# Linear attention: the newest gates' cumulative sum, moved behind the slot's outputs and queued behind the two parts of the decayed state

## The chip, the cores and the metric

The kernel runs on one core of a Trainium2 chip. A core has a matrix engine (PE in the profile; PEld is its weight load), a vector engine (DVE), a scalar engine (ACT), GpSimd (POOL, hardly used here) and SyncE (SP), which issues the DMAs. Each engine runs its own list of instructions, and semaphores order them against each other. The metric is the device time of one execution in microseconds (us).

## What is computed

One layer of an encoder block on a sequence of 1024 tokens, width 1024: a projection, a gated linear attention in both directions (GLA), a windowed attention (SWA), their output projections and a feed-forward block. The change lies in the GLA. Cut to it, the reference reads:

```python
def _gla_direction(q, k, v, log_g, include_diag):
    ...
    b = jnp.cumsum(log_g, axis=3)
    b_last = b[:, :, :, -1:, :]
    q_dec = q * jnp.exp(b)
    k_inv = k * jnp.exp(-b)
    k_tail = k * jnp.exp(b_last - b)
    scores = jnp.where(mask, jnp.einsum("bhncd,bhnmd->bhncm", q_dec, k_inv), 0.0)
    o_intra = jnp.einsum("bhncm,bhnme->bhnce", scores, v)
    chunk_kv = jnp.einsum("bhnmd,bhnme->nbhde", k_tail, v)
    def step(state, inp):
        kv_n, dec_n = inp
        return dec_n[..., None] * state + kv_n, state
    _, states = lax.scan(step, ...)
    o_inter = jnp.einsum("bhncd,nbhde->bhnce", q_dec, states)
    return (o_intra + o_inter).reshape(bsz, s, dv)
```

The gates are `log_g = max(log_sigmoid(z) / 16, -0.5)`. There are four heads, with 128 key and 256 value channels.

## The kernel before

**Number format.** Matrix products of full precision are made of three fp32r products: each operand is split into a high part (ACT copies it to fp32r) and a low part (DVE subtracts the high part), and `mm3` (L75) multiplies high by high, high by low and low by high. So nearly every operand costs one ACT and one DVE instruction before PE can use it.

**Slots.** The GLA runs as a software pipeline of slots t (loop at L627). Chunks of 128 tokens are numbered n = 8*head + c over the four heads, and go in pairs (even c and the next). What is done for chunk n stands in these slots:

- slot n, even n: `g_gates` (L399) for the pair. PE multiplies the gates' codes to `z`; ACT takes an exponential (L419), DVE clips it (L420), ACT takes the logarithm (L421), and DVE forms the cumulative sum along the tokens (L422, a scan of 128x512) and the three small rows `sm` from it (L425, L426) that give the chunks' decays.
- same slot, recorded last: `g_decays` (L430). DVE subtracts the reference points (L437, L438), ACT takes two exponentials in place (L440, L441), DVE multiplies them with k and q (`en` L443, and `G` L444). `G` has one buffer.
- slot n+1, recorded last: `g_parts` (L446): the high and low parts `kh`, `kl`, `q2f`, `q2b`.
- slot n+3: `g_scores` (L458): transposes of `en`, parts `kth` and `ktl` of them (L475, L476), the scores, ACT's copy `sp` of them (L483), the masked copy (L484), and the parts `sh` and `sl` (L487, L488).
- slot n+4: `g_out` (L493) for each chunk, in four steps: six matmuls to `kv` (128x256 each); DVE's new state `pf` (L502, or L506 at a head's first chunk), ACT's copy `kb` of the other direction (L504); the **decayed state's two parts**, `th` on ACT (L514) and `tl` on DVE (L515); and the output `o`, made of `sh`, `sl` and, from the second chunk on, the previous chunk's `th` and `tl`, which ACT copies to `ob` (L522).
- later slots: `g_back_out` (L539) and `g_back` (L524) run the other direction backwards (`thb` L533, `tlb` L534, `kb` L536, `ob` L544), and `g_turn` (L559) transposes the outputs (`ot`, L565).

Between these stages `fill` (L258) puts matmuls of the other projections: 34 in a slot up to t = 7, 21 up to t = 23, 18 up to t = 35, then 11 (`GF`, L24). Their weights need `wh` (ACT, L67) and `wl` (DVE, L69). DVE also has `x_sums` (L576, L581), side work for a later stage.

**What sets the order.** PE's order is the order in which the code is written (`manual_schedule`, L625). The order on ACT, DVE and SP is decided at build time by a scheduler that starts from the recorded order; at run time each of these engines takes its instructions in that fixed order. PSUM tiles of the GLA come from a ring of four buffers (`chtile`, L49): a new one can be written when the one four before it has been read.

Of the kernel before, what the change touches and what calls it, by code (L numbers as in the profile page):

```python
# [8 lines left out]
F32 = mybir.dt.float32  # L9
FR = mybir.dt.float32r  # L10
U32 = mybir.dt.uint32
AF = mybir.ActivationFunctionType
ALU = mybir.AluOpType
# [6 lines left out]
NC = 8  # L20
# [10 lines left out]
def body(tc, i, out):  # L31
    nc = tc.nc
    with ExitStack() as root:
# [15 lines left out]
        def chtile(shape, dt=F32):  # L49
            return psc.tile(list(shape), dt, tag="ch", name=nm("ch"))  # L50
# [21 lines left out]
        def mm(o, a, b, start, stop):  # L72
            nc.tensor.matmul(o, a, b, start=start, stop=stop)  # L73

        def mm3(o, ah, al, bh, bl, start, stop):  # L75
            mm(o, ah, bh, start, False)
            mm(o, ah, bl, False, False)
            mm(o, al, bh, False, stop)
# [191 lines left out]
        def need(key):  # L270
            while key not in scr:
                fill(12)
# [118 lines left out]
        def gtile(tag, shape=(P, 256), dt=F32, bufs=2):  # L391
            return gt.tile(list(shape), dt, tag=tag, name=nm(tag), bufs=bufs)
# [2 lines left out]
            pass  # L395

        gla = {}

        def g_gates(hd, c):  # L399


            pr = Chunk()
            for j in range(2):
                a = gla[hd, c + j] = Chunk()
                a.pr, a.j, a.t = pr, j, slice(j * P, (j + 1) * P)
            s, co = c // 4, (c % 4) * P
            for nme in ("q", "k"):
                need((f"{nme}{hd}", s))
            qk = gtile("qk", (P, 2, 256))
            nc.sync.dma_start(out=qk[:, 0], in_=scr[f"q{hd}", s][:, co:co + 256])  # L410
            nc.sync.dma_start(out=qk[:, 1], in_=scr[f"k{hd}", s][:, co:co + 256])
            z = chtile((P, 2, 256))
            for d in range(2):
                mm(z[:, d], upS[:, d, hd * P:(hd + 1) * P], lrS[:, c * P:(c + 2) * P], True, True)
            G = gtile("G", (P, 4, 2, P), bufs=1)
            Gt = G.rearrange("p a j t -> p a (j t)")
            Gf = G.rearrange("p a j t -> p (a j t)")
            cs, e, csf, ef = G[:, 0:2], G[:, 2:4], Gf[:, 0:512], Gf[:, 512:1024]
            nc.scalar.activation(ef, z.rearrange("p d t -> p (d t)"), AF.Exp, scale=-1.0)  # L419
            nc.vector.tensor_scalar(ef, ef, float(np.expm1(8.0)), None, op0=ALU.min)  # L420
            nc.scalar.activation(ef, ef, AF.Ln, bias=ones[:, 0:1])  # L421
            nc.vector.tensor_tensor_scan(csf, mask.rearrange("p c t -> p (c t)"), ef, 0.0, op0=ALU.mult, op1=ALU.add)  # L422

            pr.sm = gtile("sm", (P, 2, 2, 2), bufs=16)
            nc.vector.tensor_scalar(pr.sm, cs[:, :, :, 63:128:64], -1.0 / 16, None, op0=ALU.mult)  # L425
            nc.vector.tensor_tensor(pr.sm[:, :, :, 1], pr.sm[:, :, :, 1], pr.sm[:, :, :, 0], op=ALU.subtract)  # L426

            pr.qk, pr.G = qk, G

        def g_decays(hd, c):  # L430
            pr = gla[hd, c].pr
            qk, G = pr.qk, pr.G
            Gt = G.rearrange("p a j t -> p a (j t)")
            Gf = G.rearrange("p a j t -> p (a j t)")
            cs, e, csf, ef = G[:, 0:2], G[:, 2:4], Gf[:, 0:512], Gf[:, 512:1024]
            late = bass.AP(Gf.tensor, Gf.offset, [list(Gf.ap[0]), [255, 2], [P, 2], [1, P]])
            nc.vector.tensor_tensor(e, late, cs[:, :, :, 63:64].to_broadcast([P, 2, 2, P]), op=ALU.subtract)  # L437
            nc.vector.tensor_scalar(e[:, 1, :, 0:1], cs[:, 1, :, 63:64], -1.0, None, op0=ALU.mult)  # L438

            nc.scalar.activation(csf, ef, AF.Exp, scale=-1.0 / 16)  # L440
            nc.scalar.activation(ef, ef, AF.Exp, scale=1.0 / 16)  # L441
            pr.en = gtile("en", (P, 2, 256))
            nc.vector.tensor_tensor(pr.en, Gt[:, 1:3], qk[:, 1:2].to_broadcast([P, 2, 256]), op=ALU.mult)  # L443
            nc.vector.tensor_tensor(Gt[:, 0:4:3], Gt[:, 0:4:3], qk[:, 0:1].to_broadcast([P, 2, 256]), op=ALU.mult)  # L444
# [48 lines left out]
        def g_out(hd, c):  # L493

            a = gla[hd, c]
            kv = chtile((P, 2, 256))
            for d in range(2):
                mm3(kv[:, d], a.kth[:, d], a.ktl[:, d], a.vh, a.vl, True, True)
            a.pf = gtile("pf")
            if c:  # L500
                pf, dec, th, tl = a.before
                nc.vector.scalar_tensor_tensor(a.pf, pf, dec[:, 0:1], kv[:, 0], op0=ALU.mult, op1=ALU.add)  # L502
                a.kb = gtile(f"kb{c}", bufs=2 if c < 5 else 1)
                nc.scalar.copy(a.kb, kv[:, 1])  # L504
            else:
                nc.vector.tensor_copy(a.pf, kv[:, 0])  # L506
                a.kb = None
            if c < NC - 1:
                n = gla[hd, c + 1]
                dec2 = gtile("dec", (P, 1))  # L510
                nc.scalar.activation(dec2, n.pr.sm[:, 0, n.j, 0:1], AF.Exp, bias=a.pr.sm[:, 0, a.j, 1:2])
                th2 = gtile("th", dt=FR)
                tl2 = gtile("tl", dt=FR)
                nc.scalar.activation(th2, a.pf, AF.Copy, scale=dec2[:, 0:1])  # L514
                nc.vector.scalar_tensor_tensor(tl2, a.pf, dec2[:, 0:1], th2.bitcast(F32), op0=ALU.mult, op1=ALU.subtract)  # L515
                n.before = a.pf, dec2, th2, tl2
            o = chtile((P, 256))
            mm3(o, a.sh, a.sl, a.vh, a.vl, True, c == 0)
            if c:
                mm3(o, a.pr.q2[0][:, 0, a.t], a.pr.q2[0][:, 1, a.t], th, tl, False, True)  # L520
            a.ob = gtile(f"ob{c}", bufs=2 if c < 5 else 1)
            nc.scalar.copy(a.ob, o)  # L522

        def g_back(hd, c):  # L524

            a = gla[hd, c]
            if c < NC - 1:
                n = gla[hd, c + 1]
                dec = gtile("decb", (P, 1))
                nc.scalar.activation(dec, a.pr.sm[:, 1, a.j, 1:2], AF.Exp, bias=n.pr.sm[:, 1, n.j, 0:1])  # L530
                th = gtile("thb", dt=FR)
                tl = gtile("tlb", dt=FR)
                nc.scalar.activation(th, n.kb, AF.Copy, scale=dec[:, 0:1])  # L533
                nc.vector.scalar_tensor_tensor(tl, n.kb, dec[:, 0:1], th.bitcast(F32), op0=ALU.mult, op1=ALU.subtract)  # L534
                if c:
                    nc.vector.scalar_tensor_tensor(a.kb, n.kb, dec[:, 0:1], a.kb, op0=ALU.mult, op1=ALU.add)  # L536
                a.thb, a.tlb = th, tl
# [74 lines left out]
        for n in range(NH * NC):  # L612
            hd, c = divmod(n, NC)
            cb = hd * NC + NC + 4 + (NC - 1 - c)
            tt = cb + c % 2 + 2
            for j, (t, f) in enumerate(((n, g_gates), (n + 3, g_scores), (n + 4, g_out),
                                        (cb, g_back_out), (tt, g_turn))):
                if j > 1 or c % 2 == 0:
                    at[t, j + (j == 4 and c % 2)] = (f, hd, c)
                last = max(last, t)  # L620
            if c % 2 == 0:
                behind[n] = (g_decays, hd, c)
                behind[n + 1] = (g_parts, hd, c)
# [198 lines left out]
        for n in range(2 * KT):  # L822
            t, g = divmod(n, 2)
# [9 lines left out]
        order = (prep, a_rope, a_scores, a_turn, k_turn, a_out, a_probs)  # L833
# [91 lines left out]
        def pair_T3(f):  # L925
            nme, m, a, b = PAIRS[f]
            g = pend[f]
            product(g.X, wsplit(g.s3, 512), XT["T3"], 4, False, True)
            return result((f"{nme}{m + 4}", 1), g.X, g.p5)
# [69 lines left out]
        with tc.manual_schedule(engines={mybir.EngineType.PE}):  # L999
# [15 lines left out]
            for j in range(0, len(PAIRS), 2):  # L1015
# [4 lines left out]
                v = [pair_T3(f) for f in two]  # L1020
# [561 lines left out]
```

## Time and profile before

| | us |
|---|---|
| time, median of 3 runs (1623.01 to 1624.67) | 1623.91 |
| the profiled execution's own time | 1624.31 |
| its span in the profile | 1622.5 |
| the GLA's slots in it, about | 48 to 338 |
| DVE busy over the span | 1223.9 |
| ACT busy over the span | 915.0 |

The span is 1.8 us shorter than the profiled execution's own time, and that time is 0.4 us above the median. A group of the profile gives source line, engine, operation, output and inputs, shapes, count, busy time and the mean of one instruction in ns, and behind the bar the time for which the engine stood idle just before them and what ended it. A row of the timeline gives the start, the duration and the instruction; brackets give the idle time before it and who ended it. Matmuls are pipelined: one shown with 0.28 us lets the next start after 0.12 us, so waits of PE are read from the distance of the starts.

### The profile page before, as it was taken

To read this page: it belongs to the slowest core of one execution; us is meant where nothing else is said; L and a number is where in the kernel's file an instruction comes from. 1 tells how busy PE (TensorE), PEld (TensorE's weight loads), DVE (VectorE), ACT (ScalarE), POOL (GpSimd) and SP (SyncE) were. 2 spreads that over 40 slices of the span, in tenths; PEclk is the share of its full clock that TensorE was granted. 3 is DMA by queue.
4 is the path that set the end of the run, shared out by engine and by line. 5 is a ranking of instruction groups with operands and counts; after the bars stand their busy time and mean duration, and the time that the engine had idled before them with its cause. 6 is when DMAs were issued, how large, how long until landed. Compare 5 with 4: busy or idle time off the path is not lost.

```text
span 1622.5 us, 23392 instructions
## 1 busy us (share of the span) xinstructions
PE 1611.6 (99%) x7644; PEld 1341.5 (83%) x7644; DVE 1223.9 (75%) x2315; ACT 915.0 (56%) x1883; POOL 0.2 (0%) x4
## 2 busy tenths in 40 slices
PE   9999999999999999999999999999999999999999
PEld 7888888888888888888888888888888888888887
DVE  8568888845999777876855878677777888789655
ACT  7456777873999745445732547754444444354442
POOL 0000000000000000000000000000000000000000
PEclk9999999999999999999999999999999999999999
DMA  8855757878554487878842656643435564695433
GB/s 279 295 180 194 252 172 256 274 264 284 176 162 143 129 268 253 270 242 263 282 126 89 192 192 214 196 141 124 136 121 177 170 219 146 207 328 189 149 98 117
DMA packets 196362, 323.25 MB, mean 199 GB/s; under 512 B 22318, under 2 KB 47790, under 8 KB 196240
## 3 DMA queue, kind: packets, MB, share of 16 engines
q1 hardware_dynamic: 196240, 321.76, 60.8%
q8 instruction: 60, 0.98, 0.2%
q14 instruction: 62, 0.51, 0.1%
HBM read 216.29 MB, written 105.38 MB: 198 GB/s over the span
## 4 chain that ended last, share of the span: by engine, by line
PE 89%; DVE 4%; ACT 3%; DMA 2%; issue 1%; SPq 0%; DVEq 0%; ACTq 0%
PE mm L73 20%; PE mm L877 10%; PE mm L879 10%; PE mm L878 10%; PE mm L1421 7%; PE ch L73 7%; PE ch L1421 6%; PE ch L878 5%; PE ch L879 5%; PE ch L877 5%; PE mm L246 3%; PE ch L783 1%; DMA kvr<-skv 1%; DMA st<-in_xT_dram 1%; DVE wl L69 0%
## 5 line engine op out<-in xcount | busy, mean ns | idle before, releaser
L856 ACT ACTIVATE wh<-ws 128x512 fp32r<-128x512 f32 x164 | 102.9, 629 | 152.5 <-PE mm L878 81.0
L73 PE MATMUL mm<-wh,xh 128*128 128x512 f32 x320 | 127.1, 397 | 0.0
L73 PE MATMUL mm<-wh,xl 128*128 128x512 f32 x320 | 127.1, 397 | 0.0
L73 PE MATMUL mm<-wl,xh 128*128 128x512 f32 x320 | 126.6, 395 | 0.0
L857 DVE TENSOR_TENSOR wl<-ws,wh 128x512 fp32r<-128x512 f32 x164 | 112.2, 686 | 14.0 <-ACT wh L856 13.5
L67 ACT ACTIVATE wh<-wr 128x512 fp32r<-128x512 f32 x118 | 73.5, 627 | 53.0 <-PE mm L73 21.3
L69 DVE TENSOR_TENSOR wl<-wr,wh 128x512 fp32r<-128x512 f32 x118 | 80.8, 686 | 25.2 <-ACT wh L67 22.8
L856 ACT ACTIVATE wh<-a 128x512 fp32r<-128x512 f32 x66 | 41.6, 632 | 89.1 <-PE ch L1421 42.3
L856 ACT ACTIVATE wh<-wr 128x512 fp32r<-128x512 f32 x76 | 47.8, 631 | 58.1 <-PE mm L878 17.6
L857 DVE TENSOR_TENSOR wl<-a,wh 128x512 fp32r<-128x512 f32 x66 | 45.5, 690 | 39.7 <-ACT wh L856 39.3
L1421 PE MATMUL mm<-hh,wl 128*128 128x512 f32 x176 | 68.6, 390 | 0.0
L1421 PE MATMUL mm<-hl,wh 128*128 128x512 f32 x176 | 68.5, 389 | 0.0
L1421 PE MATMUL mm<-hh,wh 128*128 128x512 f32 x176 | 68.5, 389 | 0.0
L73 PEld LDWEIGHTS mm<-wl,xh 128*128 128x128 f32 x320 | 60.2, 188 | 9.8
L73 PEld LDWEIGHTS mm<-wh,xl 128*128 128x128 f32 x320 | 60.2, 188 | 9.6
L73 PEld LDWEIGHTS mm<-wh,xh 128*128 128x128 f32 x320 | 60.3, 188 | 9.1 <-DVE st L141 0.2
L857 DVE TENSOR_TENSOR wl<-wr,wh 128x512 fp32r<-128x512 f32 x76 | 52.0, 685 | 7.8 <-ACT wh L856 7.1
L870 DVE TENSOR_TENSOR ws<-wr,wr 128x512 f32<-128x512 f32 x80 | 54.5, 687 | 4.3 <-DMA wr<-in_w_f_dram 1.7
L1388 DVE TENSOR_TENSOR hl<-hr,hh 128x512 fp32r<-128x512 f32 x77 | 52.8, 686 | 5.7 <-ACT hh L1387 5.4
L1387 ACT ACTIVATE hh<-hr 128x512 fp32r<-128x512 f32 x77 | 47.7, 619 | 9.0 <-DMA hr<-B 5.1
L1421 PE MATMUL ch<-hh,wh 128*128 128x512 f32 x132 | 51.3, 389 | 0.0
L1421 PE MATMUL ch<-hl,wh 128*128 128x512 f32 x132 | 51.3, 389 | 0.0
(454 smaller groups left out, 4984.5 us busy)
## 6 DMA issues: line engine op xcount, KB each, us to landing
wr<-in_w_fi_dram SPq DMA_DIRECT2D x110, 256.0 KB, 3.9
wr<-in_w_f_dram SPq DMA_DIRECT2D x100, 256.0 KB, 3.7
wh<-wh SPq DMA_DIRECT2D x80, 256.0 KB, 3.1
wl<-wl SPq DMA_DIRECT2D x80, 256.0 KB, 3.1
B<-c SPq DMA_DIRECT2D x44, 256.0 KB, 2.1
T<-st SPq DMA_DIRECT2D x44, 256.0 KB, 2.9
a<-in_w_fo_dram SPq DMA_DIRECT2D x44, 256.0 KB, 5.3
hr<-T SPq DMA_DIRECT2D x44, 256.0 KB, 2.7
```

The costliest lines, as they stand in the source:

```text
L67: nc.scalar.activation(h, raw, AF.Copy)
L69: nc.vector.tensor_tensor(l, raw, h.bitcast(F32), op=ALU.subtract)
L73: nc.tensor.matmul(o, a, b, start=start, stop=stop)
L246: nc.tensor.matmul(Y[q], w[:, c], x, start=f0, stop=f1, skip_group_check=True)
L856: nc.scalar.activation(h, src, AF.Copy)
L857: nc.vector.tensor_tensor(l, src, h.bitcast(F32), op=ALU.subtract)
L870: nc.vector.tensor_tensor(t, x, y, op=op)
L877: nc.tensor.matmul(o, h[:, c], x[kk][0], start=start and kk == 0, stop=False, skip_group_check=True)
L878: nc.tensor.matmul(o, h[:, c], x[kk][1], start=False, stop=False, skip_group_check=True)
L879: nc.tensor.matmul(o, l[:, c], x[kk][0], start=False, stop=kk == nk - 1, skip_group_check=True)
L1388: nc.vector.tensor_tensor(l, r, h.bitcast(F32), op=ALU.subtract)
L1421: nc.tensor.matmul(ys[m], a[:, c], b, start=f0, stop=f1, skip_group_check=True)
```

## The change

The scan and the two `sm` instructions leave `g_gates` and open the new `g_sums`, which holds the body of `g_decays`. `g_decays` is recorded where it was, last in the even slot, behind `g_out` of that slot; so the scan is now recorded behind `g_out` too. While `g_sums` is recorded, `issue_after` makes each of its instructions on ACT follow the newest `th` on ACT's queue, and each on DVE follow the newest `tl` on DVE's queue (`state` holds the two; it is empty until the first `g_out`, so the first two pairs have no such edge). No instruction is added or left out.

```diff
         gla = {}
+        state = []
 ...
             nc.scalar.activation(ef, ef, AF.Ln, bias=ones[:, 0:1])
-            nc.vector.tensor_tensor_scan(csf, mask.rearrange("p c t -> p (c t)"), ef, 0.0, op0=ALU.mult, op1=ALU.add)
-
-            pr.sm = gtile("sm", (P, 2, 2, 2), bufs=16)
-            nc.vector.tensor_scalar(pr.sm, cs[:, :, :, 63:128:64], -1.0 / 16, None, op0=ALU.mult)
-            nc.vector.tensor_tensor(pr.sm[:, :, :, 1], pr.sm[:, :, :, 1], pr.sm[:, :, :, 0], op=ALU.subtract)
-
             pr.qk, pr.G = qk, G

         def g_decays(hd, c):
-            pr = gla[hd, c].pr
+            with ExitStack() as order:
+                for v in state:
+                    order.enter_context(tc.issue_after(v.ins))
+                g_sums(gla[hd, c].pr)
+
+        def g_sums(pr):
             qk, G = pr.qk, pr.G
 ...
+            nc.vector.tensor_tensor_scan(csf, mask.rearrange("p c t -> p (c t)"), ef, 0.0, op0=ALU.mult, op1=ALU.add)
+
+            pr.sm = gtile("sm", (P, 2, 2, 2), bufs=16)
+            nc.vector.tensor_scalar(pr.sm, cs[:, :, :, 63:128:64], -1.0 / 16, None, op0=ALU.mult)
+            nc.vector.tensor_tensor(pr.sm[:, :, :, 1], pr.sm[:, :, :, 1], pr.sm[:, :, :, 0], op=ALU.subtract)
+
             late = bass.AP(Gf.tensor, Gf.offset, [list(Gf.ap[0]), [255, 2], [P, 2], [1, P]])
 ...
-                nc.scalar.activation(th2, a.pf, AF.Copy, scale=dec2[:, 0:1])
-                nc.vector.scalar_tensor_tensor(tl2, a.pf, dec2[:, 0:1], th2.bitcast(F32), op0=ALU.mult, op1=ALU.subtract)
+                v1 = nc.scalar.activation(th2, a.pf, AF.Copy, scale=dec2[:, 0:1])
+                v2 = nc.vector.scalar_tensor_tensor(tl2, a.pf, dec2[:, 0:1], th2.bitcast(F32), op0=ALU.mult, op1=ALU.subtract)
 ...
             nc.scalar.copy(a.ob, o)
+            if c < NC - 1:
+                state[:] = v1, v2
```

PE's order is the same before and after. On the other engines the scheduler's order changes from the third pair on until the end of the GLA. Three places of it follow, all around slot t = 28, in which the gates of the pair 28, 29 are made and head 3's first chunk gives its output. (Line numbers after the change are 1 to 14 higher: the scan L422 becomes L436, `th` L514 becomes L520, `tl` L515 becomes L521, `ob` L522 becomes L528, the exponentials L440, L441 become L446, L447.)

On DVE in slot t = 28, from the low part `sl` of the scores on, before the change:

```order
L488 TENSOR_TENSOR sl_3769<-sp_3765,sh_3768 128x256
L420 TENSOR_SCALAR G_3799<-G_3799 128x512
L422 SCALAR_TENSOR_TENSOR G_3799<-mask,G_3799 128x512
L425 TENSOR_SCALAR sm_3804<-G_3799 128x8
L437 TENSOR_TENSOR G_3799<-G_3799 128x512
L426 TENSOR_TENSOR sm_3804<-sm_3804 128x4
L506 COPY pf_3844<-ch_3837 128x256
L438 TENSOR_SCALAR G_3799<-G_3799 128x2
L69 TENSOR_TENSOR wl_3891<-wr_3887,wh_3889 128x512
L515 SCALAR_TENSOR_TENSOR tl_3849<-pf_3844,dec_3846,th_3848 128x256
```

The same place after the change:

```order
L494 TENSOR_TENSOR sl_3769<-sp_3765,sh_3768 128x256
L421 TENSOR_SCALAR G_3799<-G_3799 128x512
L544 SCALAR_TENSOR_TENSOR kb_725_3361<-kb_750_3465,decb_4066,kb_725_3361 128x256
L544 SCALAR_TENSOR_TENSOR kb_678_3162<-kb_725_3361,decb_4164,kb_678_3162 128x256
L512 COPY pf_3840<-ch_3833 128x256
L521 SCALAR_TENSOR_TENSOR tl_3845<-pf_3840,dec_3842,th_3844 128x256
L436 SCALAR_TENSOR_TENSOR G_3799<-mask,G_3799 128x512
L69 TENSOR_TENSOR wl_3891<-wr_3887,wh_3889 128x512
L439 TENSOR_SCALAR sm_3855<-G_3799 128x8
L443 TENSOR_TENSOR G_3799<-G_3799 128x512
```

The state `pf` and its part `tl` moved ahead of the scan and the subtraction; two updates of `kb` (another direction's state) moved behind `sl`.

On ACT in the same slot, from the gates' logarithm on, before:

```order
L421 ACTIVATE G_3799<-G_3799,ones 128x512
L221 ACTIVATE st_3832<-mm_3285,rstdt 128x512
L67 ACTIVATE wh_3889<-wr_3887 128x512
L514 ACTIVATE th_3848<-pf_3844,dec_3846 128x256
L440 ACTIVATE G_3799<-G_3799 128x512
L221 ACTIVATE st_3870<-mm_3286,rstdt 128x512
L441 ACTIVATE G_3799<-G_3799 128x512
L522 COPY ob_852_3856<-ch_3852 128x256
L565 COPY ot_3907<-ch_3904 128x256
```

And after:

```order
L422 ACTIVATE G_3799<-G_3799,ones 128x512
L221 ACTIVATE st_3828<-mm_3285,rstdt 128x512
L520 ACTIVATE th_3844<-pf_3840,dec_3842 128x256
L67 ACTIVATE wh_3889<-wr_3887 128x512
L221 ACTIVATE st_3870<-mm_3286,rstdt 128x512
L573 COPY ot_3907<-ch_3904 128x256
L67 ACTIVATE wh_4051<-wr_4049 128x512
L528 COPY ob_851_3852<-ch_3848 128x256
L573 COPY ot_3917<-ch_3914 128x256
L446 ACTIVATE G_3799<-G_3799 128x512
```

The output's copy `ob`, which frees a PSUM buffer, stood behind both exponentials and stands ahead of both now.

On DVE at the end of the slot before (t = 27), from `ktl` to `sl`, before:

```order
L476 TENSOR_TENSOR ktl_3749<-ch_3743,kth_3748 128x512
L536 SCALAR_TENSOR_TENSOR kb_750_3465<-kb_789_3608,decb_3930,kb_750_3465 128x256
L534 SCALAR_TENSOR_TENSOR tlb_3933<-kb_789_3608,decb_3930,thb_3932 128x256
L536 SCALAR_TENSOR_TENSOR kb_726_3365<-kb_750_3465,decb_4070,kb_726_3365 128x256
L484 COPY_PREDICATED sp_3765<-tri,ch_3752 128x256
L536 SCALAR_TENSOR_TENSOR kb_678_3162<-kb_726_3365,decb_4164,kb_678_3162 128x256
L487 CAST sh_3768<-sp_3765 128x256
L488 TENSOR_TENSOR sl_3769<-sp_3765,sh_3768 128x256
```

And after:

```order
L482 TENSOR_TENSOR ktl_3749<-ch_3743,kth_3748 128x512
L462 TENSOR_TENSOR q2f_3776<-G_3555,q2f_3776 128x256
L462 TENSOR_TENSOR q2b_833_3777<-G_3555,q2b_833_3777 128x256
L589 TENSOR_TENSOR xn_3648<-xn_3648,xn_3546 128x512
L542 SCALAR_TENSOR_TENSOR tlb_3816<-kb_811_3701,decb_3813,thb_3815 128x256
L544 SCALAR_TENSOR_TENSOR kb_788_3604<-kb_811_3701,decb_3813,kb_788_3604 128x256
L490 COPY_PREDICATED sp_3765<-tri,ch_3752 128x256
L544 SCALAR_TENSOR_TENSOR kb_750_3465<-kb_788_3604,decb_3930,kb_750_3465 128x256
L493 CAST sh_3768<-sp_3765 128x256
L542 SCALAR_TENSOR_TENSOR tlb_3933<-kb_788_3604,decb_3930,thb_3932 128x256
L494 TENSOR_TENSOR sl_3769<-sp_3765,sh_3768 128x256
```

The parts `q2f` and `q2b` of the newer pair now stand between `ktl` and `sl`; two of the four updates of `kb` left the stretch ahead of `sl`.

More of the change, by code (lines that the diff above doesn't have):

```diff
@@ L421, in g_gates, with g_decays @@
             nc.scalar.activation(ef, ef, AF.Ln, bias=ones[:, 0:1])
+            pr.qk, pr.G = qk, G
+        def g_decays(hd, c):
+            with ExitStack() as order:
[3 more added lines that the diff above has]
+        def g_sums(pr):
+            qk, G = pr.qk, pr.G
+            Gt = G.rearrange("p a j t -> p a (j t)")
+            Gf = G.rearrange("p a j t -> p (a j t)")
+            cs, e, csf, ef = G[:, 0:2], G[:, 2:4], Gf[:, 0:512], Gf[:, 512:1024]
             nc.vector.tensor_tensor_scan(csf, mask.rearrange("p c t -> p (c t)"), ef, 0.0, op0=ALU.mult, op1=ALU.add)
@@ L426, in g_gates @@
             nc.vector.tensor_tensor(pr.sm[:, :, :, 1], pr.sm[:, :, :, 1], pr.sm[:, :, :, 0], op=ALU.subtract)
-            pr.qk, pr.G = qk, G
-        def g_decays(hd, c):
-            pr = gla[hd, c].pr
[L432 to L435, printed above, removed]
             late = bass.AP(Gf.tensor, Gf.offset, [list(Gf.ap[0]), [255, 2], [P, 2], [1, P]])
```

## The prediction

> **What bounds the kernel now.** The page first: busy times, and by engine the chain that ended last.
>
> ```profile
> PE 1611.6 (99%) x7644; PEld 1341.5 (83%) x7644; DVE 1223.9 (75%) x2315; ACT 915.0 (56%) x1883; POOL 0.2 (0%) x4
> PE 89%; DVE 4%; ACT 3%; DMA 2%; issue 1%; SPq 0%; DVEq 0%; ACTq 0%
> ```
>
> PE bounds the kernel, and the change alters neither its instructions nor their order. So the change is worth the time for which PE stands still in the GLA's slots, no more, plus whatever new waits it makes there. The table by stretches shows how much slack the helpers have (columns: stretch, its length, then busy time and count of PE, PEld, DVE, ACT, POOL, clock, DMA share, GB/s).
>
> ```profile
> 125.00:200.00 75.00, 75.00 (x441) 65.51 (x440) 64.31 (x146) 52.27 (x138) 0.00 (x0) 1.00 0.70 228
> 260.00:320.00 60.00, 58.09 (x348) 50.12 (x347) 53.50 (x126) 49.09 (x138) 0.00 (x0) 1.00 0.78 255
> ```
>
> DVE is 86% busy in the first and 89% in the second, where a slot holds fewer filling matmuls; ACT goes from 70% to 82%. The granted clock is 1.00 throughout. The waits between 45 and 345 us name who holds PE (total, times, longest):
>
> ```profile
> PE ch L73 <- ACT ob L522: 1.4, 2, 1.1
> PE ch L73 <- DVE sh L487: 0.8, 2, 0.6
> ```
>
> Only idle time between modelled ends counts there. The true loss is read from the starts of PE's rows. Undisturbed, the 9 matmuls of a head's first `g_out` take 1.07 us and the 12 of a later one 1.43 us, as the chain's rows show (and a 512-wide filling matmul 3.88 / 17 = 0.23 us):
>
> ```profile
> 85.80 1.07 PE ch L73 x9
> 86.88 3.88 PE mm L73 x17
> 90.75 1.43 PE ch L73 x12
> ```
>
> Below, for the five places where it takes longer, the rows of the timeline that enclose it.
>
> ```profile
> 216.37 0.28 PE L73 MATMUL ch<-vh,kth 128*128 128x256 f32 x1
> ...
> 218.06 0.39 PE L73 MATMUL mm<-wl,xh 128*128 128x512 f32 x1
> ...
> 223.39 0.32 PE L73 MATMUL ch<-vh,kth 128*128 128x256 f32 x1
> ...
> 225.45 0.40 PE L73 MATMUL mm<-xh,wl 128*128 128x512 f32 x1
> ...
> 285.14 0.28 PE L73 MATMUL ch<-vh,kth 128*128 128x256 f32 x1
> ...
> 286.86 0.40 PE L73 MATMUL mm<-wh,xl 128*128 128x512 f32 x1
> ...
> 291.14 0.40 PE L73 MATMUL mm<-wh,xl 128*128 128x512 f32 x1
> 292.62 0.39 PE L73 MATMUL ch<-vh,kth 128*128 128x256 f32 x1 [1.08 <-ACT ob L522]
> ...
> 294.15 0.40 PE L73 MATMUL mm<-wh,xh 128*128 128x512 f32 x1
> ...
> 314.63 0.28 PE L73 MATMUL ch<-vh,kth 128*128 128x256 f32 x1
> ...
> 317.02 0.40 PE L73 MATMUL mm<-wh,xl 128*128 128x512 f32 x1
> ```
>
> The losses: t = 20, 218.06 - 216.37 - 1.07 = 0.62 (waits for `sh`, `sl`); t = 21, 225.45 - 223.39 - 1.43 = 0.63 (for `ob`); t = 28, 1.72 - 1.07 = 0.65 (`sh`, `sl`); t = 29, 294.15 - 291.14 - 1.43 - 0.23 (the filling matmul) = 1.35 (`ob`); t = 32, 2.39 - 1.43 = 0.96 (`sh`). Together **4.2 us, 0.26%** of the time: the most that the change can gain, unless it moves something outside the GLA, whose orders it leaves alone. A difference under 0.2%, 3.25 us here, is about what a measurement of this kernel can't tell from no change.
>
> **The change part by part.** Nothing is added or removed; there are no DMAs in the moved step, and SP keeps its 1364 instructions with some loads swapped. So it's all a matter of what waits behind what.
>
> *The copies `ob` (t = 21, 29).* ACT's rows in slot t = 28:
>
> ```profile
> 290.18 0.51 ACT L514 ACTIVATE th<-pf,dec 128x256 fp32r<-128x256 f32 x1 [1.41 <-DVE pf L506]
> ...
> 291.68 0.62 ACT L441 ACTIVATE G<-G 128x512 f32<-128x512 f32 x1
> 292.20 0.36 ACT L522 COPY ob<-ch 128x256 f32<-128x256 f32 x1
> ```
>
> and DVE's:
>
> ```profile
> 286.16 0.43 DVE L488 TENSOR_TENSOR sl<-sp,sh 128x256 fp32r<-128x256 f32 x1
> ...
> 287.71 1.22 DVE L422 TENSOR_TENSOR_SCAN G<-mask,G 128x512 f32<-128x512 f32 x1 [0.79 <-ACT G L421]
> ...
> 289.73 0.42 DVE L506 COPY pf<-ch 128x256 f32<-128x256 f32 x1
> ...
> 290.73 0.48 DVE L515 SCALAR_TENSOR_TENSOR tl<-pf,dec,th 128x256 fp32r<-128x256 f32 x1
> ...
> 292.33 0.69 DVE L443 TENSOR_TENSOR en<-G,qk 128x512 f32<-128x512 f32 x1 [0.46 <-ACT G L441]
> ```
>
> PE had finished `o` by 286.86 plus a matmul's length. The copy waited until 292.20: ACT stood 1.41 us for `pf`, which was queued on DVE behind the scan, and then ran `th` and both exponentials ahead of the copy. After the change `pf` follows `sl`, L420 and two `kb` updates at about 287.8 (`sl` ends at 286.59; the three at 0.4 of DVE's time each), 1.9 us earlier, and on ACT neither exponential is ahead of the copy. `pf` and `th` take 0.42 + 0.51, to 288.7; left ahead of the copy are two `wh` and an `st`, as large as an exponential (0.62), and an `ot`, as large as the copy (0.36): at most 2.2 us. So `ob` starts by 290.9 instead of 292.20 and ends by 291.3; PE wants the buffer at 291.14 + 0.23 = 291.37. Gain 1.35 at t = 29, and by the same order 0.63 at t = 21: **-1.98**.
>
> *The scan's delay, and `sl` (t = 20, 28).* The scan now waits for `pf`, `th` and `tl`. These last:
>
> ```profile
> L502 DVE SCALAR_TENSOR_TENSOR pf<-pf,dec,ch 128x256 f32<-128x256 f32 x28 | 13.3, 476 | 0.5 <-PE ch L73 0.4
> L515 DVE SCALAR_TENSOR_TENSOR tl<-pf,dec,th 128x256 fp32r<-128x256 f32 x28 | 13.5, 483 | 8.6 <-ACT th L514 8.6
> ```
>
> So the scan starts up to 0.48 + 0.51 + 0.48 = 1.5 us later. Whether that reaches the scores is worked through in slots t = 26 and 27, whose `sl` is the one that PE waited for at t = 28. DVE's rows before:
>
> ```profile
> 272.01 1.22 DVE L422 TENSOR_TENSOR_SCAN G<-mask,G 128x512 f32<-128x512 f32 x1
> ...
> 275.35 0.48 DVE L515 SCALAR_TENSOR_TENSOR tl<-pf,dec,th 128x256 fp32r<-128x256 f32 x1 [0.77 <-ACT th L514]
> 276.66 0.69 DVE L69 TENSOR_TENSOR wl<-wr,wh 128x512 fp32r<-128x512 f32 x1 [0.83 <-ACT wh L67]
> 277.27 0.69 DVE L443 TENSOR_TENSOR en<-G,qk 128x512 f32<-128x512 f32 x1
> ...
> 278.47 0.41 DVE L544 TENSOR_TENSOR ob<-ob,ch 128x256 f32<-128x256 f32 x1
> ...
> 285.44 0.48 DVE L536 SCALAR_TENSOR_TENSOR kb<-kb,decb,kb 128x256 f32<-128x256 f32 x1
> ```
>
> After: scan at 272.01 + 1.5 = 273.5; it takes 1.22, the `wl` behind it 0.69, L425 and L437 with L426 0.8 (in t = 28, from the scan's end at 288.93 to `pf` at 289.73), L438 0.1, the two exponentials 2 x 0.62: `en` at 277.5, 0.2 later than before. The delay is nearly absorbed, since the two idle times of 0.77 and 0.83 in this stretch fall away. From `en` to the end of `sl` DVE took 286.59 - 277.27 = 9.3 us. Of that two updates of `kb` (0.48 shown, about 0.4 to the next start, each) now stand behind `sl` and the addition to `ob` (0.33 to the next start) ahead of `en`. So `sl` ends at 277.5 + 9.3 - 1.1 = 285.7, 0.9 earlier; PE reaches `sh` at 285.14 + 6 x 0.12 = 285.85. The stop goes. At t = 20 the same shift of about 0.9 covers 0.62. Bounds: the delay reaches `sl` whole (+1.5) or `sl` gains 1.1 without any delay; I take the worked value. Together **-1.27**.
>
> *The stop at t = 32.* PE arrives there 1.98 + 1.27 = 3.25 earlier than before, DVE's chain does not by itself: the gates behind it (t = 30) come with PE, but their scan takes the delay of 1.5, and the order there frees about 1.1. I keep the stop and add the rest: **+0.4**.
>
> *Other slots.* PE comes earlier into slots whose `sl` had some time in hand. The two with the least, beside those counted, are at t = 22 and 30:
>
> ```profile
> 232.43 0.42 DVE L488 TENSOR_TENSOR sl<-sp,sh 128x256 fp32r<-128x256 f32 x1
> ...
> 233.84 0.28 PE L73 MATMUL ch<-vh,sh 128*128 128x256 f32 x1
> ...
> 300.87 0.42 DVE L488 TENSOR_TENSOR sl<-sp,sh 128x256 fp32r<-128x256 f32 x1
> ...
> 301.85 0.28 PE L73 MATMUL ch<-vh,sh 128*128 128x256 f32 x1
> ```
>
> PE needs `sl` two matmuls behind `sh`: 233.84 + 0.24 - 232.85 = 1.2 us in hand at t = 22, 301.85 + 0.24 - 301.29 = 0.8 at t = 30. Zero to 1 us of new stops in all; I take **+0.3**. `sm` is up to 1.5 later at no cost: its first reader (`dec` of a chunk's `g_out`) runs three slots on, and two slots last 15.7 us (scan to scan, 272.01 to 287.71). `q2b`, after which the next gates may overwrite `G`, is covered by the rest of slot n+1; if that cover were gone, the excess would be added to the scan's delay, as in rival C.
>
> Sum: -1.98 - 1.27 + 0.4 + 0.3 = **-2.55**. The profiled execution took 1624.31, so 1621.76; it lay 0.40 above the median, so on the median's scale 1621.4.
>
> **The rivals.**
>
> *A: every stop goes,* that of t = 32 too. For it: `en` hardly moves and `sl` gains everywhere. Against it: PE's five stops were time that DVE, 89% busy, used as well. -4.2: 1619.7.
>
> *B: hidden anyway.* DVE, not PE's waits, sets the pace from t = 20 on, and what is won at one stop is lost at the next `sl`. For it: the stops for `sh` and `sl` recur three times at 89%. Against it: DVE still has 6.5 us idle in those 60, and the `ob` stops are ACT's order, not work. It keeps a quarter of the `ob` gain: -0.5, 1623.4.
>
> *C: late scores.* The scan's 1.5 us reaches `sl` whole in each slot from t = 20 on. Three slots had nothing in hand (3 x 1.5 = 4.5 us), t = 30 had 0.8 (0.7 us lost) and t = 22 1.2 (0.3 us): +5.5 - 1.98 = +3.5, 1627.4. It turns to a loss when more than about 0.66 us of delay arrives (3 x 0.66 = 1.98). For it: DVE is the busiest helper, and the scan, ready at 272.01, is made to wait for ACT. Against it: the idle times that the delay can use. The Trainium skill, page "PSUM — Partial Sum Buffer", section "Engine vs sequencer instructions", says that the queues of ScalarE and VectorE are strict FIFOs, so an instruction queued behind a waiting one waits as well; by that rule taken alone the scan and all behind it stand for `th`, which is C, +3.5 instead of -2.55. The trace agrees with the rule (the `ob` copy at 292.20 stood behind work that it didn't need), but by the same rule the old order held up `pf`, `th` and `ob`.
>
> *D: the change doesn't take.* The orders show the scan behind `tl`; only the first two pairs keep their place. No chance of its own.
>
> **How the numbers follow.** Forecast 0.47, A 0.18, B 0.23, C 0.12. Faster by over 0.2% (under 1620.7): A and a part of the forecast, 0.25. Slower by over 0.2% (over 1627.2): most of C and nothing else, 0.09. Within: 0.66. The range reaches from a little below A (1619.5) to 1625.2: that is C's mechanism with 1 us of delay arriving (3 x 1 + 0.2 - 1.98 = +1.2). It takes in B and leaves out most of C.
>
> **What would show it.** In the changed profile PE's waits for `ob` are gone, and the rows at t = 21 and 29 are 1.43 long. ACT's `th` idles less than 1.4 for `pf` at a head's first chunk. The scan begins 0.5 to 2 us behind `kv` and DVE's wait for `th` before `tl` grows. `sl` ends 0.5 to 1 us earlier against PE's `kv` at t = 20 and 28. The GLA's last transposes come about 2.5 us earlier, and everything behind is shifted by that. Wrong I'd be if PE shows new stops for `sh` of over 1 us at t = 22 to 30, or if a later stage waits for something that isn't paced by PE.

## The result and the profile after

The changed kernel takes **1631.98 us** (median of 6 executions, 1630.35 to 1633.22) against 1624.13 for the kernel before (6, 1622.91 to 1624.67): a ratio of **1.0048**, 95% interval 1.0038 to 1.0058. It is 6 to 9 us slower, where 1621.4 was forecast and the range ended at 1625.2. The profiled execution took 1631.12 us, 6.8 more than that of before; its span is 1629.3.

Line numbers behind the moved code are 6 to 8 higher now: the scan is L436, `th` and `tl` L520 and L521, `ob` L528, `sh` and `sl` L493 and L494, the exponentials L446 and L447, `en` L449. The eviction `st` keeps L141. First PE's waits between 45 and 345 us of the changed kernel (who waits, for whom; total, times, longest):

```profile
PE mm L73 <- DVE st L141: 2.8, 1, 2.8
PE ch L73 <- DVE sh L493: 2.3, 3, 1.9
PE ch L73 <- DVE sl L494: 0.6, 3, 0.3
```

The waits for `ob` (1.4 us before) are gone, as forecast. Those for `sh` and `sl` have grown from 1.0 us (0.8 and, in the line below, 0.2) to 2.9.

```profile
PE ch L73 <- DVE sl L488: 0.2, 1, 0.2
```

On top of the changed kernel's list stands a wait that no view of the kernel before shows: a filling matmul waits for `st`, DVE's eviction of a finished projection. PE's timeline at that place:

```profile
152.44 0.40 PE L73 MATMUL mm<-wh,xl 128*128 128x512 f32 x1
155.63 0.50 PE L73 MATMUL mm<-wh,xh 128*128 128x512 f32 x1 [2.80 <-DVE st L141]
155.97 0.39 PE L73 MATMUL mm<-wl,xh 128*128 128x512 f32 x1
...
157.16 0.63 PE L73 MATMUL mm<-wh,xl 128*128 128x512 f32 x1
157.59 0.63 PE L73 MATMUL mm<-wh,xh 128*128 128x512 f32 x1
...
159.30 0.41 PE L73 MATMUL ch<-vh,kth 128*128 128x256 f32 x1
```

Start to start, the stop is 155.63 - 152.44 - 0.23 = **2.96 us** (2.97 in the expectations below). About 1.1 us after PE goes on, matmuls that take 0.23 us elsewhere come 0.43 us apart, six of them: another 6 x 0.20 = **1.2 us**. The table by stretches says why (the changed kernel first, then one row of the kernel before; stretch, its length, busy time and count of PE, PEld, DVE, ACT, POOL, granted clock, DMA share, GB/s):

```profile
155.00:157.00 2.00, 1.37 (x5) 1.13 (x6) 2.00 (x5) 0.14 (x1) 0.00 (x0) 0.89 0.63 241
157.00:159.40 2.40, 2.40 (x7) 1.83 (x7) 1.30 (x3) 1.01 (x2) 0.00 (x0) 0.50 0.84 262
159.40:162.00 2.60, 2.60 (x16) 2.40 (x15) 1.43 (x3) 1.47 (x4) 0.00 (x0) 0.89 0.92 340
```

```profile
157.00:159.40 2.40, 2.40 (x14) 2.04 (x14) 2.40 (x8) 0.68 (x2) 0.00 (x0) 1.00 0.43 164
```

The granted clock, 1.00 in the same stretches of the kernel before, falls to 0.50 behind the stop. PE "busy 2.40 of 2.40" there is PE at half speed. The other matmuls of the slow stretch, the 256-wide ones above all, lose some 0.4 us more: the matmul that starts at 155.89 in the kernel before starts at 160.91 here, 5.0 us later with all that came ahead of it.

**Why the eviction is late.** The projections accumulate in a ring of four PSUM tiles (`mmtile`). The projection that starts at 149.66 us (values of the third and fourth heads) uses all four, and its third and fourth tile hold the finished keys of the third head, k2, until DVE has evicted them. The first matmul into the third tile is the 13th of the projection, the one that stops at 155.63. In DVE's timeline of the changed kernel (slots t = 10 and 11):

```profile
138.74 0.75 DVE L584 SCALAR_TENSOR_TENSOR xn<-xn,g,rstd 128x512 f32<-128x512 f32 x1 [0.78 <-DMA xn<-in_xT_dram]
...
140.34 0.42 DVE L421 TENSOR_SCALAR G<-G 128x512 f32<-128x512 f32 x1
142.08 0.69 DVE L69 TENSOR_TENSOR wl<-wr,wh 128x512 fp32r<-128x512 f32 x1 [1.31 <-ACT wh L67]
142.69 0.47 DVE L508 SCALAR_TENSOR_TENSOR pf<-pf,dec,ch 128x256 f32<-128x256 f32 x1
...
144.01 0.48 DVE L521 SCALAR_TENSOR_TENSOR tl<-pf,dec,th 128x256 fp32r<-128x256 f32 x1 [0.24 <-ACT th L520]
144.41 1.22 DVE L436 TENSOR_TENSOR_SCAN G<-mask,G 128x512 f32<-128x512 f32 x1
...
148.05 0.69 DVE L449 TENSOR_TENSOR en<-G,qk 128x512 f32<-128x512 f32 x1 [1.04 <-ACT G L447]
...
154.89 0.68 DVE L141 TENSOR_TENSOR st<-mm,rstd 128x512 f32<-128x512 f32 x1
```

and the same work before:

```profile
138.23 0.42 DVE L420 TENSOR_SCALAR G<-G 128x512 f32<-128x512 f32 x1
139.44 1.23 DVE L422 TENSOR_TENSOR_SCAN G<-mask,G 128x512 f32<-128x512 f32 x1 [0.79 <-ACT G L421]
...
144.00 0.69 DVE L443 TENSOR_TENSOR en<-G,qk 128x512 f32<-128x512 f32 x1 [0.40 <-ACT G L441]
...
151.45 0.68 DVE L141 TENSOR_TENSOR st<-mm,rstd 128x512 f32<-128x512 f32 x1
```

From `en` to `st` DVE works almost without a break in both (7.45 us before, 6.84 after), so `st` is late because `en` is late. The scan used to run as soon as its gates were there, at 139.44, while PE was still at `kv` (139.11 to 139.98). Now it stands behind `tl`, the exponentials behind the scan, and DVE idles 1.04 us for them. Of the scan's 5.0 us 2.1 are there ahead of the edge: the clip of its gates (L420, now L421) comes at 140.34 instead of 138.23, behind work left over from the slots before and 0.78 us of waiting for a load. In PE's time (it had lost 0.4 us by 149.66) the eviction comes 3.44 - 0.38 = 3.1 us later. It had next to nothing in hand, as PE's timeline of the kernel before shows: the eviction is over at 152.13, and the 13th matmul of the projection, into the freed tile, is the one at 152.30. So nearly all of the 3.1 us became PE's stop.

```profile
152.06 0.40 PE L73 MATMUL mm<-wh,xl 128*128 128x512 f32 x1
152.30 0.40 PE L73 MATMUL mm<-wh,xh 128*128 128x512 f32 x1
```

**The end of the GLA.** In slot t = 32, where PE lost 0.96 us before, the `kv` matmuls are done and `sh` is not there:

```profile
319.29 0.28 PE L73 MATMUL ch<-vh,ktl 128*128 128x256 f32 x1
321.43 0.36 PE L73 MATMUL ch<-vh,sh 128*128 128x256 f32 x1 [1.86 <-DVE sh L493]
...
322.07 0.38 PE L73 MATMUL ch<-vh,sl 128*128 128x256 f32 x1 [0.17 <-DVE sl L494]
```

2.0 us for `sh`, 0.4 for what follows it. With 0.5 to 0.9 us at t = 22, 28 and 30 and 0.3 at 316 us the late stops come to some 4.9 us, against 4.2 before, of which 2.0 were the stops for `ob`. Matmul by matmul, PE's lag behind the kernel before grows by 0.6 us from t = 20 to the end of t = 32. So the GLA's account in this pair of executions is: early +0.4 (for `tl`, at 144.55) + 2.96 + 1.2 + 0.4, late +0.6, together **+5.6 of 6.8 us**. Another 0.9 is at one matmul of SWA (458 us), whose stop lies between 0.2 and 1.6 us in the traces of this study and follows no edit that I can see. The rest, 0.3, is a sum of gains and losses of up to 0.7 us in later stages that no run here explains.

### The profile page after: what moved, and what is told of

It is laid out like the page before. It is cut to its first block, busy times and chain, and to the rows that moved or that the text cites. A ratio compares the mean times of both kernels' runs of the same rounds, so it can differ in the third digit from the quotient of the medians.

```text
span 1629.3 us, 23407 instructions
## 1 busy us (share of the span) xinstructions
PE 1614.8 (99%) x7644; PEld 1343.9 (82%) x7644; DVE 1221.2 (75%) x2315; ACT 916.6 (56%) x1883; POOL 0.2 (0%) x4
## 4 chain that ended last, share of the span: by engine, by line
PE 87%; DVE 5%; ACT 4%; DMA 2%; issue 1%; SPq 0%; DVEq 0%; ACTq 0%
PE mm L73 19%; PE mm L887 10%; PE mm L885 10%; PE mm L886 10%; PE mm L1429 7%; PE ch L73 6%; PE ch L1429 6%; PE ch L887 5%; PE ch L886 5%; PE ch L885 5%; PE mm L246 3%; PE ch L791 1%; ACT p L774 1%; ACT p L780 1%; DMA kvr<-skv 1%
## 5 line engine op out<-in xcount | busy, mean ns | idle before, releaser
L1429 PE MATMUL ch<-hh,wl 128*128 128x512 f32 x132 | 51.4, 389 | 0.0
```

The costliest lines, as they stand in the source:

```text
L1429: nc.tensor.matmul(ys[m], a[:, c], b, start=f0, stop=f1, skip_group_check=True)
```

## Experiments

Every kernel below was timed beside the kernel before on the same chip in five rounds. The medians of before in the three groups are 1623.77, 1624.29 and 1624.16 us; the ratios count. Stops and waits are those of the one profiled execution, times and ratios those of all. None leaves out any of the computation.

### The place in the program, the one slot, the heads

For the next kernels the moved lines (scan and `sm`) become a function `g_scan`, and a condition says for which pairs the change holds:

```diff
+        def moved(hd, c):
+            return hd * NC + c != 10
         def g_gates(hd, c):
...
             pr.qk, pr.G = qk, G
+            if not moved(hd, c):
+                g_scan(pr)
         def g_decays(hd, c):
             with ExitStack() as order:
-                for v in state:
+                for v in state if moved(hd, c) else ():
                     order.enter_context(tc.issue_after(v.ins))
```

In the expectations the projection whose eviction is late is called k1; it is k2.

**Without the edges** (`for v in state` and its `with` dropped, all else as changed):

> The change without its two order edges: the cumulative sum is still written behind the slot's outputs, but nothing is queued behind th and tl. Theory (the edges do it: the scan, whose gates are ready before the matmuls kv, has to stand for kv, pf, th and tl): the scan starts within 1.5 us of where it stood before, no pause of PE for st near 155 us, time 1622.5 to 1626. Rival (the place in the program does it, since it decides what DVE takes first): a pause of 2 us or more at the same projection and 1630 or more.

Measured: 1625.11 us, ratio 1.0009 (1.0000 to 1.0018); wait for `st` 0.4 us, waits for `ob` 1.3. The scan stands within 0.4 us of its old place in every pair. So the recorded place is worth little, and the edges make the loss.

**All but t = 10:**

> The change everywhere but in slot t = 10 (second head, chunk 2), whose scan is written and queued as before. Theory (one place: the scan of t = 10 comes 5.0 us late, DVE's eviction of the projection k1 then 3.4 us late, PE stops 2.97 us for a free buffer and the six matmuls after it lose 1.2 us at a lower clock): that pause and the slow matmuls are gone, time 1631.98 - 4.2 = 1627.8, between 1627 and 1628.6. Rival (DVE is late in every slot and the pause only shows where a projection ends): PE pauses as long at another place and the time stays at 1631 or more.

Measured: 1629.77 us, ratio 1.0032 (1.0020 to 1.0043). That is over both expectations. The stop for `st` shrinks to 1.2 us, start to start, and no stretch behind it has a lower clock, but it isn't gone. (The profiled execution, 1627.19 us, was the fastest of six; in two of the others the mean clock was below 1.00.)

**t = 10 alone:**

> The change in slot t = 10 alone, all other pairs as before. Theory (one place): the pause of about 3 us and the slow matmuls behind it come back, 1624.13 + 4.2 = 1628.3. Rival (the delay is built up over the pairs t = 4, 6 and 8 before it): a pause under 1 us and 1624 to 1625.5.

Measured: 1625.06 us, ratio 1.0008 (0.9999 to 1.0017), a stop of 1.2 us for `st` at full clock. Neither theory of these two holds alone. The delay of t = 10 and that which the pairs before it leave behind make a stop of 1.2 us each, and only together 2.96 and the slow clock. One place, fed by several pairs.

**t = 20 and 28 alone** (condition `hd * NC + c in (20, 28)`):

> The change in slots t = 20 and 28 alone, where PE stopped for ob a slot later. Theory (the ob term of the prediction was right, the scores' term wrong: the scan stands for kv there, and sl comes later, not earlier): the ob stops of 0.63 and 1.35 us go, and up to 1.5 us of new waits for sh and sl come at t = 22 and 30: 1622 to 1624. Rival (my forecast's step: sl gains too): 1624.13 - 1.98 = 1622.1 or less and no new wait. Second rival (ob's gain is lost whole at the next sl): 1624 to 1626.

Measured: 1624.50 us, ratio 1.0003 (0.9994 to 1.0012). PE's waits:

```profile
PE ch L73 <- ACT kb L521: 0.9, 1, 0.9
PE ch L73 <- DVE sh L504: 0.8, 2, 0.5
PE ch L73 <- DVE sl L505: 0.5, 2, 0.4
```

The `ob` waits go, 1.4 us, and a new one for `kb` and longer ones for `sl` give it back: the second rival.

### Which wait: `kv`, `th` or the exponentials

Next to the times I need how late DVE's chain is. For each of the 14 moved pairs I took the start of `scan`, `en` and `sl` less that of the first `kv` matmul of the slot in the same trace, and subtracted the kernel before's. For t = 26 that matmul starts at 271.17 and 275.28 us, the scan at 272.01 and 278.78: 3.50 - 0.84 = 2.66 us late. The means of this and DVE's total wait for `th` ahead of `tl` between 45 and 345 us:

| kernel | scan | en | sl | wait for th | ratio |
|---|---|---|---|---|---|
| before | 0 | 0 | 0 | 8.6 | 1 |
| changed | +3.4 | +3.0 | +1.2 | 11.9 | 1.0048 |
| edges, scan not moved | +0.1 | +1.9 | +0.8 | 11.3 | 1.0037 |
| scan behind `pf` only | +1.6 | +1.2 | -0.3 | 2.5 | 0.9996 |
| edge behind `th` only | 0.0 | +0.5 | -0.1 | 9.1 | 1.0001 |
| no edges | +0.1 | +0.1 | +0.1 | 8.1 | 1.0009 |

**Scan behind `pf`:**

```diff
-                nc.vector.scalar_tensor_tensor(a.pf, pf, dec[:, 0:1], kv[:, 0], op0=ALU.mult, op1=ALU.add)
+                v1 = nc.vector.scalar_tensor_tensor(a.pf, pf, dec[:, 0:1], kv[:, 0], op0=ALU.mult, op1=ALU.add)
...
-                state[:] = v1, v2
+                state[:] = v1,
```

> The change with one edge in place of two: the cumulative sum is queued behind the update of the state (pf, on DVE) alone, not behind th and tl. Theory (the scan's delay is the wait for PE's matmuls kv, which pf reads; th and tl add only their own 1.0 us): the scan stands 1 us earlier than in the changed kernel, the pause for st stays at 1.5 to 2.5 us, time 1628 to 1631. Rival (the trip through ACT, th then tl, is the delay): pause under 0.6 us and 1624 to 1626.

Measured: 1623.85 us, ratio **0.9996** (0.9987 to 1.0005). My theory fell: with the wait for `kv` still in place the loss is gone. It leaves half of the scan's delay (1.6 of 3.4 us) and the stop for `st` at 1.45 us, against the rival's 0.6, without a slow matmul behind it, but `sl` is on time in the mean, and the `ob` stops are gone, which pays for the rest. What the other order does is in this kernel's DVE timeline:

```profile
141.88 0.48 DVE L508 SCALAR_TENSOR_TENSOR pf<-pf,dec,ch 128x256 f32<-128x256 f32 x1
142.27 1.22 DVE L436 TENSOR_TENSOR_SCAN G<-mask,G 128x512 f32<-128x512 f32 x1
143.41 0.67 DVE L589 TENSOR_TENSOR xn<-xn,xn 128x512 f32<-128x512 f32 x1
143.99 0.48 DVE L521 SCALAR_TENSOR_TENSOR tl<-pf,dec,th 128x256 fp32r<-128x256 f32 x1
```

`tl` needs `th`, and `th` is a trip from DVE to ACT and back. The scan fills that trip, and `tl` finds `th` ready. The waits of DVE, this kernel first, then the changed one:

```profile
DVE tl L521 <- ACT th L520: 2.5, 3, 0.8
```

```profile
DVE wl L69 <- ACT wh L67: 17.2, 12, 3.3
DVE tl L521 <- ACT th L520: 11.9, 16, 0.9
```

**The edges without the move** (the scan and `sm` back in `g_gates`, the rest of `g_decays` behind `th` and `tl`):

> The two edges alone: cumulative sum and sm where they were, and only the rest of the decays (the subtraction L437 and what follows on DVE, the exponentials on ACT) queued behind tl and th. Theory (the cost is the wait of DVE's chain for kv, pf, th and tl, the scan's own 1.22 us being only a part): the chain is 1.2 us less late than in the changed kernel, the pause for st 1 to 2 us, time 1626.5 to 1629.5. Rival one (all of the delay is the scan's): 1624 to 1625.5. Rival two (the scan's place is of no account): 1631 or more.

Measured: 1630.63 us, ratio 1.0037 (1.0025 to 1.0050), over the expected times. `en` is 1.1 us less late than in the changed kernel, about the scan's own length, as expected, and the stop for `st` 1.65 us. But the late part loses more than in the changed kernel (PE's lag grows by 2.4 us from 200 to 330 us, there by 0.6):

```profile
PE ch L73 <- DVE sh L493: 1.6, 2, 1.4
PE mm L73 <- DVE st L141: 1.5, 1, 1.5
PE ch L73 <- ACT ob L528: 1.1, 2, 0.6
PE ch L73 <- DVE ob L552: 0.9, 2, 0.7
```

As I read it, the scan, early again, holds up `pf` and so `ob`, and the subtraction, late, holds up the scores: both costs and little of either gain.

**The edge behind `th` alone** (`state[:] = v1,`):

> The change with the edge behind th alone: on ACT the exponentials stay queued behind th, on DVE the cumulative sum is queued behind nothing. Theory (the price is DVE's queue: with the sum behind tl, nothing fills DVE's wait for th; with the sum free or behind pf, it does): scan and en stand as in the kernel before to within 1 us, no stop of over 1 us for st, 1623 to 1625.5. Rival (the exponentials' place behind th makes the scores late): en later by 2 us or more, 1628 or more.

Measured: 1624.10 us, ratio 1.0001 (0.9992 to 1.0010). `en` is up to 1.8 us late in single slots, but PE shows no new stop of over 0.4 us in the GLA: the exponentials' place on ACT costs nothing that can be measured. The other half needs no run: with the edge behind `tl` alone the program is, instruction for instruction, the changed one. The whole loss hangs on the edge behind `tl`.

### The clock behind a stop

The kernel before, with the first eviction of k2 done six times over:

```diff
-                    nc.vector.tensor_tensor(t, b[s], rstd[:, s * HT:(s + 1) * HT], op=ALU.mult)
+                    for _ in range(6 if name == "k2" and s == 0 else 1):
+                        nc.vector.tensor_tensor(t, b[s], rstd[:, s * HT:(s + 1) * HT], op=ALU.mult)
```

> The kernel before, with DVE's eviction of the first half of the projection k2 done six times over into the same buffer, so that it ends some 3 us or more later and nothing else is moved. Theory (a pause of PE of about 3 us makes the clock fall after it): PE pauses 2.5 to 4 us for st near 155 us, six or so matmuls behind the pause are spaced 0.43 us instead of 0.23, and the time is 1623.8 + pause + 1.2, some 1628. Rival (the slow matmuls come from something else in the changed kernel): a pause as long, with matmuls at 0.23 us behind it, 1626 to 1627.

Measured: 1627.76 us, ratio 1.0024 (1.0014 to 1.0033). In the profiled execution PE stops 2.2 us, less than the 2.5 to 4 expected, and then once more, since both evictions of k2 are late now:

```profile
154.49 0.50 PE L73 MATMUL mm<-wh,xh 128*128 128x512 f32 x1 [2.04 <-DVE st L142]
...
155.59 0.63 PE L73 MATMUL mm<-wl,xh 128*128 128x512 f32 x1
156.02 0.63 PE L73 MATMUL mm<-wh,xl 128*128 128x512 f32 x1
157.22 0.80 PE L73 MATMUL mm<-wh,xh 128*128 128x512 f32 x1 [0.58 <-DVE st L142]
157.82 0.63 PE L73 MATMUL mm<-wl,xh 128*128 128x512 f32 x1
```

```profile
155.00:157.00 2.00, 1.65 (x5) 0.72 (x4) 2.00 (x5) 0.72 (x1) 0.00 (x0) 0.61 0.34 131
157.00:159.40 2.40, 2.18 (x6) 1.79 (x7) 2.40 (x5) 0.49 (x1) 0.00 (x0) 0.50 0.79 253
159.40:162.00 2.60, 2.60 (x12) 2.41 (x12) 1.38 (x5) 0.88 (x4) 0.00 (x0) 0.50 0.70 270
```

The clock falls to 0.50 here too, with the GLA's order untouched: the slow stretch follows from the stop. It falls ahead of the second stop (the matmuls at 155.59 and 156.02 are 0.43 us apart), so the first, of 2.2 us, was enough. The mean clock of the whole execution was under 1.00 in 8 of these 10 executions and in all 6 of the changed kernel, against 4 of the 75 of the kernel before in the three groups.

### The gain by itself, and a faster kernel

**`ob` first, nothing moved on DVE** (edges on ACT only, in t = 20 and 28):

```diff
+            copy = nc.scalar.copy(a.ob, o)
+            if c < NC - 1:
+                state[:] = [copy] if hd >= 2 and c == 0 else []
...
-                nc.scalar.activation(th2, a.pf, AF.Copy, scale=dec2[:, 0:1])
+                with tc.issue_after(copy.ins) if hd >= 2 and c == 0 else nullcontext():
+                    nc.scalar.activation(th2, a.pf, AF.Copy, scale=dec2[:, 0:1])
```

> The kernel before, with nothing moved on DVE: only in slots t = 20 and 28 the copy ob is recorded ahead of th, and th and the two exponentials are queued behind it on ACT. Theory (the ob stops were ACT's order alone): both ob stops (0.63 and 1.35 us) go, the exponentials are not later than before by more than 0.5 us, time 1621.8 to 1622.8. Rival (as in the change, what PE gains there it gives back at the next sh, sl): 1623.5 to 1625.

Measured: 1622.15 us, ratio 0.9992 (0.9983 to 1.0000). Both `ob` waits are gone and no longer wait stands in their place; from 215 to 340 us PE gains 1.6 us, start to start, on the kernel before:

```profile
PE ch L73 <- DVE sh L494: 0.8, 2, 0.5
PE ch L73 <- DVE sl L495: 0.2, 1, 0.2
```

**Early and late pairs apart.** The change as it is for `hd * NC + c < 18`, and the scan behind `pf` for `hd * NC + c >= 18`:

> The change as it is (queued behind th and tl), in the pairs up to t = 16 alone; the pairs t = 18 to 30 as before. Theory (the early part's price is the pause for st and the clock behind it, 2.97 + 1.2 us; the late part's is the stops for sh and sl less the ob gain): the pause of 3 us and the slow matmuls are there, the ob stops at t = 21 and 29 stay, 1628 to 1629. Rival (DVE's lateness carries over from the early into the late pairs): 1630 or more.

Measured: 1630.02 us, ratio 1.0037 (1.0023 to 1.0050), a stop of 2.98 us for `st` with slow matmuls behind it, the `ob` stops back, `en` and `sl` from t = 20 on as before to 0.3 us. That time lies in the rival's range, but the trace is against it: from 200 to 340 us PE's lag behind the kernel before changes by less than 0.3 us. Little carries over, then, and most of the changed kernel's loss, 1.0037 of 1.0048, is made by the pairs up to t = 16. The late pairs' share is the difference, some 1.8 us, which these intervals don't resolve.

> The sum moved and queued behind pf only, as in the run with one edge to pf, but in the pairs t = 18 to 30 alone; the pairs up to t = 16 as before. Theory (that run paid 1.45 us for st at the early pairs and won about 2 at the ob stops and sl of the late ones): no stop for st near 155 us, no ob stops, 1621 to 1623. Rival (its late pairs gain nothing, the gain was the noise of a run): 1623.5 to 1625.

Measured: 1622.67 us, ratio **0.9990** (0.9981 to 0.9999). The gain is under the 0.2% that the prediction took for the limit of what can be told from no change, so the time alone doesn't show it; the trace does, with 1.6 us that PE gains from 215 to 340 us. PE's waits are down to

```profile
PE ch L73 <- DVE ob L563: 0.9, 2, 0.6
PE ch L73 <- DVE sh L504: 0.5, 1, 0.5
```

## Why the prediction was wrong, step by step

- **PE bounds, and the stops are 4.2 us.** Right, and the cap on the gain with it. But the stops of the kernel before cap only the gain. The loss is capped by nothing that they show.
- **The `ob` copies, -1.98.** Right: the waits went, and with ACT's order alone most of that gain shows in the trace (1.6 us; ratio 0.9992).
- **The scan's delay: the step that failed.** "The scan now waits for `pf`, `th` and `tl` ... So the scan starts up to 0.48 + 0.51 + 0.48 = 1.5 us later", and "the delay is nearly absorbed". Measured: 1.7 to 5.0 us late, 3.4 in the mean. I added up instruction lengths and left out the waits between them: that for `kv` on PE (DVE's waits for it ahead of `pf` grew from 0.4 to 5.7 us), and the trip to ACT, behind whatever stands in both queues. Half of it (1.6) is there with the scan behind `pf`, the other half (1.8) comes with `th` and `tl`. In the very slot that I worked through (t = 26) the scan came 2.7 and `en` 1.5 us late, not 0.2.
- **"The two idle times ... fall away."** The opposite: DVE's wait for `th` rose from 8.6 to 11.9 us and that for `wh` (11.2 before) to 17.2. The scan was what DVE did in such gaps. Queued behind the instruction that waits, it can't fill its wait.
- **`sl`, -1.27.** Wrong in size and partly in sign. It is 1.2 us later in the mean; the stop at t = 20 went, that at t = 28 grew from 0.65 to 0.9, t = 30 gained one of 0.8, and t = 32 went from 0.96 to 2.4 (+1.5, not +0.4).
- **"Other slots", +0.3.** The term that was mis-sized most: +5.0, at t = 10 and 11. I priced only `sl` and only in the slots from t = 20 on. What else DVE frees for PE, the evictions `st`, I did not look at, though the rows at 151.45 and 152.30 show that this one had 0.2 us in hand.
- **"The granted clock is 1.00 throughout."** True of the kernel before, and not of the changed one: 0.50 for some 3.4 us, some 1.6 us of the loss.
- **The rivals.** C had the sign and the mechanism (late chain, FIFO) and 0.12 of the chance. Its place was wrong: it looked from t = 20 on, where the net loss is +0.6 us in the traces, not +3.5. The rule on FIFO queues that I weighed with it was the one to follow: "by that rule taken alone the scan and all behind it stand for `th`" is what the edge behind `tl` did. The signs that I gave were half of them right: the `ob` waits went and the wait for `th` grew, but the scan starts 2.6 to 5.8 us behind `kv`, not 0.5 to 2. The sign that I named for being wrong, new stops for `sh` of over 1 us at t = 22 to 30, didn't come (0.9 at most): the loss lay where I had named no sign.

## What to carry to other kernels

An instruction that was ready early may be the filler of another's wait. Before it is queued behind something, list the waits that it fills and what it releases; put it behind the producer of the trip (`pf`), not behind the consumer (`tl`), and it still fills it. A delay on a helper engine is to be held against *every* buffer that this engine frees for the bounding one, in each slot, with the time each has in hand, not only against the places where the bounding engine already waits: two delays that cost a stop of 1.2 us each by themselves met at one buffer, and the longer stop cost clock as well.

## What the hardware showed

A stop of the matrix engine can cost more than its length. Behind stops of 2.96, 2.98 and 2.2 us the granted clock fell to 0.50 and a 128x512 matmul took 0.43 us in place of 0.23; behind stops of 1.45, 1.65 and 2.0 us (the last at t = 32) it stayed 1.00 in the profiled executions. The clock fell about 1 us after PE had gone on. By the table it was low for (0.11 x 2.00 + 0.50 x 2.40 + 0.11 x 2.60) / 0.50 = 3.4 us, and in the kernel with two stops until about 162 us. The Trainium skill, page "TensorE: Matmul & The Clock Gate", section "Part 1: The HAM clock gate", has the clock halve after an idle window of about 3.4 us that runs freely. The half rate agrees with 0.50; the stops here were shorter than 3.4 us, and the traces can't tell how they fell into such a window.
